# Solving the delta rule's triangular systems for eight matrices at once, in 64-row quarters of TensorE

## The chip, the cores and the metric

The kernel runs on one core of one Trainium2 chip. The metric is the device time of one execution in microseconds (us). A NeuronCore has a matrix engine (TensorE, in the profile PE for its matmuls and PEld for the loading of its weights), VectorE (DVE), ScalarE (ACT) and GpSimd (POOL); SyncE (SP) starts most of the transfers. Matmul results go to PSUM, which is cut into eight banks of 512 fp32 columns.

## The reference

The program is a small decoder trunk: two layers, 512 tokens, model width 1024, fp32. Each layer normalizes x, projects it by one large matrix, and sends the parts to three mixers: a gated spatial MLP, a sliding-window attention, and a gated DeltaNet of 4 heads of 128 channels. Their outputs are projected, gated and added; a SwiGLU MLP follows. The part that the change touches is the DeltaNet. Cut to what matters, with chunks of C = 64 tokens:

```python
q, k, v, beta, g = to_chunks(q), to_chunks(k), to_chunks(v), to_chunks(beta), to_chunks(g)
gc = jnp.cumsum(g, axis=-1)
decay = jnp.exp(jnp.where(tril, gc[..., :, None] - gc[..., None, :], -jnp.inf))
k_beta = k * beta[..., None]
lower = jnp.where(strict, jnp.einsum('nbhid,nbhjd->nbhij', k_beta, k) * decay, 0.0)
a_mat = lower + jnp.eye(C, dtype=jnp.float32)
rhs = jnp.concatenate([v * beta[..., None], k_beta * jnp.exp(gc)[..., None]], axis=-1)
sol = lax.linalg.triangular_solve(a_mat, rhs, left_side=True, lower=True, unit_diagonal=True)
u_c, w_c = sol[..., :hd], sol[..., hd:]
...
def step(state, xs):
    qd, wc, uc, at, kd, cd = xs
    v_new = uc - jnp.einsum('bhcd,bhde->bhce', wc, state)
    o_c = jnp.einsum('bhcd,bhde->bhce', qd, state) + jnp.einsum('bhij,bhje->bhie', at, v_new)
    state = state * cd[..., None, None] + jnp.einsum('bhcd,bhce->bhde', kd, v_new)
    return state, o_c
```

So per head and chunk there is a unit lower triangular matrix to be inverted, and then a scan over the chunks that carries a 128x128 state.

## The kernel before, in words

**Tiling.** Tokens stand in 4 chunks of 128 (twice the reference's chunk; the result is the same by algebra). The large projections run on TensorE with 512-column outputs in four PSUM banks with the tag mm. Their fp32 operands are split into a high and a low fp32r part (hH and hL, wh and wl), and three matmuls stand for one. ScalarE makes wh from a loaded weight tile st, VectorE makes wl. Everything small (DeltaNet, attention, transposes) runs as plain fp32 matmuls into four other banks with the tag px.

**The DeltaNet.** A class Delta stands for two of the four heads (gi is 0 or 1). decay and keys build la for each chunk: la[:, hl, 0, :] is the strictly lower matrix of head hl, transposed, 128x128; keys also scales k into kd, on VectorE (line 632). queries and values prepare q and v. blocks, in one go for all 16 matrices of the layer (4 heads, 4 chunks), fetches their 16x16 diagonal blocks by a DMA into nx, inverts these on VectorE (prd and tb) and spreads the result over the partitions as cols. solve (lines 673 to 727) then builds the inverse of one pair of heads in one chunk. It starts from the 16x16 blocks in Tm and, transposed, in Uc, and has two levels, 16 and 32. At each level TensorE multiplies la by Tm for two heads into one px bank; VectorE multiplies that by a mask lmt and writes ys; TensorE multiplies ys by the other matrix; VectorE subtracts. All these matmuls are 128x128, so the two 64-row diagonal blocks go through one matmul, half of whose entries are zero. A last step joins the 64-row blocks, by 64x64 matmuls (lines 712 to 723). The result U goes to scan, which waits for it chunk by chunk: dv is updated from the state S (lines 747 to 752), U times dv gives y, which is written over la, and kd times y gives the next S.

**What sets the order.** TensorE's order is fixed by a planner (class Issue, lines 50 to 165). Each piece of work is a stream, a generator with a rank; `run` continues the first stream, by rank, whose time has come. A stream's time comes when its last result would be ready by the planner's own costs plus a latency LAT of 0.7; the large projections have rank 10 and fill what is left. Streams wait for one another by named events: a solve waits for blocks{l}, the scan for U{l}{gi}{c}. Two Delta streams (gi 0 and 1) run solve side by side, so their matmuls stand in TensorE's order as pairs. On the other engines the order is the scheduler's, by priorities; `soon()` raises that of the solve's evacuations.

The solve streams are started by these lines:

```python
for e in d:
    issue.spawn(2, dn_stream(e))
    issue.spawn(3, e.solves())
    issue.spawn(1, qv_stream(e))
```

Of the kernel before, what the change touches and what calls it, by code (L numbers as in the profile page):

```python
# [10 lines left out]
F32 = mybir.dt.float32  # L11
# [3 lines left out]
ALU = mybir.AluOpType  # L15
# [3 lines left out]
P = 128  # L19
# [8 lines left out]
HEAD_PERM = [0, 4, 1, 5, 2, 6, 3, 7]  # L28
LEVELS = [16, 32]


# [7 lines left out]
DENSE = 10  # L39
PAD = 48  # L40
SOON = 200
# [122 lines left out]
def hybrid_kernel(ctx, tc, x0, pos, wi, wkv, wb, wo, wg, wd, gn, convw, lngb, sguw, sgub,  # L164
# [33 lines left out]
    def cst(shape, name, dt=F32):  # L198
        return const.tile(shape, dt, name=name, tag=name)
# [58 lines left out]
    for b in (16, 32, 64):  # L258
        t = cst([P, P], f"blk{b}") if b == 16 else tmpc.tile([P, P], F32, name=f"blk{b}")
        v = t.rearrange("p (n b) -> p n b", b=b)  # L260
        nc.gpsimd.affine_select(v, ones.rearrange("p (n b) -> p n b", b=b), pattern=[[-b, P // b], [0, b]],
                                compare_op=ALU.is_ge, fill=0.0, base=0, channel_multiplier=1)
        nc.gpsimd.affine_select(v, v, pattern=[[b, P // b], [0, b]],
                                compare_op=ALU.is_ge, fill=0.0, base=b - 1, channel_multiplier=-1)
        blk[b] = t

    lmt = {}
    for b in LEVELS:
        t = cst([P, P], f"lmt{b}")
        nc.gpsimd.tensor_tensor(t, blk[2 * b], blk[b], ALU.subtract)  # L270
        nc.gpsimd.tensor_tensor(t, t, tri_gt, ALU.mult)
        lmt[b] = t
    blk16 = blk[16]

# [153 lines left out]
    def layer(l, norm, first=None):  # L428
# [110 lines left out]
        def h2(t):  # L539
            return t.rearrange("p (h i) -> p h i", h=2)  # L540

        def bc(m):
            return m.unsqueeze(1).broadcast_to([P, 2, P])

        def hb():
            return bank("px")[:, :256]
# [5 lines left out]
        def hs(hl):  # L552
            return slice(hl * P, (hl + 1) * P)
# [3 lines left out]
        def soon():  # L557

            return tc.high_priority(SOON)

        class Delta:
# [10 lines left out]
            def wt(self, shape, name, bufs=1):  # L572
                return self.wk.tile(shape, F32, tag=name, name=nm(name), bufs=bufs)
# [4 lines left out]
            def decay(self):  # L578

                for c in range(NCH):  # L580
                    col = self.col(c)
                    lg = self.wt([P, 2, P], "Tm", 2)
                    for hl in range(2):
# [13 lines left out]
            def keys(self):  # L597
# [4 lines left out]
                for c in range(NCH):  # L602
# [28 lines left out]
                    for hl in range(2):  # L631
                        nc.vector.tensor_scalar(self.kd[hl][:, tk], pt[:, hs(hl)], kds[:, hl:hl + 1], None, ALU.mult)
                    yield
# [26 lines left out]
            def values(self):  # L660
                for hl in range(2):
                    yield f"v{l}{2 * self.gi + hl}"
                for c in range(NCH):
# [7 lines left out]
                    yield  # L671

            def solve(self, c):

                wt, la = self.wt, self.la[c]
                m = 8 * self.gi + 2 * c
                with soon():
                    Tm, U = wt([P, 2, P], "Tm", 2), wt([P, 2, P], "Uc", 2)
                    for i, (eng, t) in enumerate(((nc.vector, Tm), (nc.gpsimd, U))):
                        eng.tensor_tensor(t.rearrange("p a (n b) -> p a n b", b=16),  # L680
                                          cols[0][:, i, m:m + 2].unsqueeze(2).broadcast_to([P, 2, 8, 16]),
                                          blk16.rearrange("p (n b) -> p n b", b=16).unsqueeze(1)
                                          .broadcast_to([P, 2, 8, 16]), ALU.mult)
                yield
                for b in LEVELS:
                    py = hb()
                    for hl in range(2):
                        nc.tensor.matmul(py[:, hs(hl)], lhsT=la[:, hl, 0, :], rhs=Tm[:, hl, :], start=True, stop=True)
                    with soon():
                        ys = wt([P, 2, P], "ys", 2)  # L690
                        nc.vector.tensor_tensor(ys, h2(py), bc(lmt[b]), ALU.mult)
                    yield
                    pz = hb()
                    if b == 16:
                        for hl in range(2):
                            nc.tensor.matmul(pz[:, hs(hl)], lhsT=U[:, hl, :], rhs=ys[:, hl, :], start=True, stop=True)
                        with soon():
                            nc.vector.tensor_tensor(Tm, Tm, h2(pz), ALU.subtract)
                            U = wt([P, 2, P], "U", 6)
                            for hl in range(2):  # L700
                                nc.vector.transpose(U[:, hl, :], Tm[:, hl, :])
                    else:
                        for hl in range(2):
                            nc.tensor.matmul(pz[:, hs(hl)], lhsT=ys[:, hl, :], rhs=U[:, hl, :], start=True, stop=True)
                        with soon():
                            nc.vector.tensor_tensor(U, U, h2(pz), ALU.subtract)
                            for hl in range(2):
                                nc.vector.transpose(Tm[32:64, hl, 0:32], U[0:32, hl, 32:64])
                    yield
                py = hb()  # L710
                for hl in range(2):
                    nc.tensor.matmul(py[64:128, hl * 64:(hl + 1) * 64], lhsT=la[0:64, hl, 0, 64:128],
                                     rhs=Tm[0:64, hl, 0:64], start=True, stop=True)
                with soon():
                    ys = wt([P, 2, P], "ys", 2)
                    nc.scalar.copy(ys[64:128, :, 0:64], py[64:128, 0:128].rearrange("p (h i) -> p h i", h=2))
                yield
                pz = hb()
                for hl in range(2):
                    nc.tensor.matmul(pz[0:64, hl * 64:(hl + 1) * 64], lhsT=ys[64:128, hl, 0:64],  # L720
                                     rhs=U[64:128, hl, 64:128], start=True, stop=True)
                with soon():
                    nc.vector.tensor_scalar(U[0:64, :, 64:128], pz[0:64, 0:128].rearrange("p (h i) -> p h i", h=2),
                                            -1.0, None, ALU.mult)
                self.U[c] = U
                issue.set(f"U{l}{self.gi}{c}")
                yield

            def solves(self):
                for c in range(NCH):  # L730
                    if c >= 3:
                        yield f"o{l}{self.gi}{c - 3}"
                    yield f"blocks{l}"
                    yield from self.solve(c)

            def scan(self):
                yield f"z{l}"
                for c in range(NCH):
# [63 lines left out]
                    issue.set(f"o{l}{self.gi}{c}")  # L802
                    yield

        def blocks(wk):
# [315 lines left out]
        for e in d:  # L1121
            issue.spawn(2, dn_stream(e))
            issue.spawn(3, e.solves())
            issue.spawn(1, qv_stream(e))
        issue.spawn(4, keys_done())
        issue.spawn(5, attn_prep())
# [266 lines left out]
```

## Time and profile before

| | us |
|---|---|
| median of 3 runs | 1744.66 (1744.47 to 1744.91) |
| profiled execution, its own time | 1743.22 |
| span of the profiled execution | 1741.5 |
| TensorE matmuls, busy | 1718.5 |
| VectorE, busy | 875.7 |
| ScalarE, busy | 638.5 |
| GpSimd, busy | 413.4 |

The span goes from the first to the last instruction of the profiled execution; its mean granted TensorE clock was 0.998 of full speed. Durations of matmuls in the timeline include the end of the pipeline, which lies beside the next matmul; what one costs is the distance to the next start. In a group, out<-in names the tiles without their numbers, and "px<-Tm,la" is a matmul that reads Tm and la into a px bank. Behind the "|" of a group stand its busy time, the mean duration in ns, and the idle time of the engine ahead of it with what ended most of that. An fp32 matmul of the solve has two records in the trace.

### The profile page before, as it was taken

Reading aid. Unit: us, or ns where it says so; the run is one execution under the profiler, and the core shown is the slowest. Engines: PE = TensorE matmul, PEld = TensorE weight load, DVE = VectorE, ACT = ScalarE, POOL = GpSimd, SP = SyncE. Lnnn points to the kernel's source line nnn. Section 1 sums busy time; section 2 is a strip of 40 time slices with the busy share of each in tenths; the row PEclk is TensorE's granted clock in tenths of the full one; section 3 lists DMA queues with packets and bytes.
Section 4 is the critical chain, followed back from the end, with each engine's and each line's share of the span. In section 5 each row is a group of like instructions: output and inputs, shape, how many; then the busy total and the mean of one; then the engine's idle time right before and its main releaser. Section 6 shows DMA issues by size and latency. Waiting matters only on the chain.

```text
span 1741.5 us, 22004 instructions
## 1 busy us (share of the span) xinstructions
PE 1718.5 (99%) x8324; PEld 1421.1 (82%) x8324; DVE 875.7 (50%) x1744; ACT 638.5 (37%) x1182; POOL 413.4 (24%) x447
## 2 busy tenths in 40 slices
PE   9999999999999999999999998999999999999998
PEld 8888778888888888888888886788888888888886
DVE  7695875454443333332266948744444433333224
ACT  7454553322333222222244455533233422222212
POOL 2424221011223333310014143210212233333000
PEclk9999999999999999999999999999999999999999
DMA  5222112222352222234332220122224434444222
GB/s 173 92 95 85 37 43 75 96 97 97 109 172 96 97 98 97 94 114 130 119 117 97 89 85 25 56 85 87 95 97 134 162 109 122 121 121 157 97 97 85
DMA packets 73115, 176.57 MB, mean 101 GB/s; under 512 B 24945, under 2 KB 25201, under 8 KB 73009
## 3 DMA queue, kind: packets, MB, share of 16 engines
q1 hardware_dynamic: 71184, 170.71, 30.3%
q0 software_dynamic: 1248, 3.41, 0.7%
q8 instruction: 65, 1.06, 0.3%
q10 hardware_dynamic: 576, 1.05, 0.2%
q14 instruction: 42, 0.34, 0.1%
HBM read 162.03 MB, written 13.11 MB: 101 GB/s over the span
## 4 chain that ended last, share of the span: by engine, by line
PE 93%; DVE 4%; DMA 1%; POOL 1%; ACT 1%; issue 1%; SPq 0%; POOLq 0%; ACTq 0%; DVEq 0%
PE mm L119 81%; PE px L119 12%; DMA nx<-blkscr 1%; DVE wl L119 0%; POOL of L119 0%; DVE zg L119 0%; DVE U L119 0%; DMA blkscr<-la 0%; DVE pr L119 0%; DVE gv L119 0%; DVE ys L119 0%; DVE gw L119 0%; DMA x<-in_x 0%; POOL pr L119 0%; DVE S L119 0%
## 5 line engine op out<-in xcount | busy, mean ns | idle before, releaser
L119 ACT CAST wh<-st 128x1024 fp32r<-128x1024 f32 (+2 forms) x286 | 295.8, 1034 | 834.0 <-PE mm L119 629.9
L119 PE MATMUL mm<-hH,wh 128*128 128x512 f32 x1344 | 532.9, 397 | 0.0
L119 PE MATMUL mm<-hH,wl 128*128 128x512 f32 x1344 | 523.8, 390 | 0.0
L119 PE MATMUL mm<-hL,wh 128*128 128x512 f32 x1344 | 523.2, 389 | 0.0
L119 DVE TENSOR_TENSOR wl<-st,wh 128x1024 fp32r<-128x1024 f32 (+2 forms) x286 | 353.1, 1235 | 220.2 <-ACT wh L119 209.5
L119 PEld LDWEIGHTS mm<-hH,wl 128*128 128x128 f32 x1344 | 252.2, 188 | 53.3
L119 PEld LDWEIGHTS mm<-hH,wh 128*128 128x128 f32 x1344 | 252.4, 188 | 52.9 <-issue 2.2
L119 PEld LDWEIGHTS mm<-hL,wh 128*128 128x128 f32 x1344 | 252.6, 188 | 51.1 <-issue 1.4
L119 POOL TENSOR_TENSOR s<-s,rep 128x512 f32<-128x512 f32 x44 | 77.3, 1756 | 162.3 <-ACT s L119 162.3
L119 POOL TENSOR_TENSOR aL<-s,aH 128x512 fp32r<-128x512 f32 x44 | 77.4, 1760 | 156.5 <-ACT aH L119 156.5
L119 POOL TENSOR_TENSOR gt<-gt,gt 128x512 f32<-128x512 f32 x32 | 48.8, 1524 | 267.8 <-DVE gt L119 267.8
L119 DVE TENSOR_TENSOR s<-mm,s 128x512 f32<-128x512 f32 x44 | 30.4, 692 | 143.9 <-PE mm L119 137.1
L119 DVE TENSOR_TENSOR s<-mm,rep 128x512 f32<-128x512 f32 x44 | 30.4, 692 | 138.3 <-PE mm L119 121.2
L119 DVE TENSOR_TENSOR gt<-mm,rep 128x512 f32<-128x512 f32 x48 | 33.1, 690 | 105.0 <-PE mm L119 105.0
L119 PE MATMUL mm<-wh,hH 128*128 128x512 f32 (+1 forms) x208 | 83.6, 402 | 0.1
L119 PE MATMUL mm<-wh,hL 128*128 128x512 f32 (+1 forms) x208 | 80.2, 386 | 0.6 <-DVE hL L119 0.6
L119 PE MATMUL mm<-wl,hH 128*128 128x512 f32 (+1 forms) x208 | 79.6, 383 | 0.0
L119 PE MATMUL mm<-brH,wh 128*128 128x512 f32 x192 | 74.7, 389 | 0.0
L119 PE MATMUL mm<-brL,wh 128*128 128x512 f32 x192 | 74.7, 389 | 0.0
L119 PE MATMUL mm<-brH,wl 128*128 128x512 f32 x192 | 74.7, 389 | 0.0
L119 PE MATMUL mm<-aH,wh 128*128 128x512 f32 x176 | 68.5, 389 | 0.0
L119 PE MATMUL mm<-aL,wh 128*128 128x512 f32 x176 | 68.5, 389 | 0.0
(285 smaller groups left out, 2494.9 us busy)
## 6 DMA issues: line engine op xcount, KB each, us to landing
st<-in_wi SPq DMA_DIRECT2D x104, 512.0 KB, 3.2
st<-in_wg SPq DMA_DIRECT2D x88, 512.0 KB, 3.3
st<-in_wb SPq DMA_DIRECT2D x24, 512.0 KB, 3.2
st<-in_wt SPq DMA_DIRECT2D x22, 512.0 KB, 3.3
st<-in_wo SPq DMA_DIRECT2D x16, 512.0 KB, 3.3
st<-in_wd SPq DMA_DIRECT2D x16, 512.0 KB, 3.5
xscr<-xt SPq DMA_DIRECT2D x24, 256.0 KB, 2.0
xt<-xscr SPq DMA_DIRECT2D x24, 256.0 KB, 2.9
```

The lines of the kernel that those rows point to most:

```text
L119: return f(*args, **kw)
```

## The change

The method solve of one pair of heads in one chunk goes; a function solves(b) takes its place, with b = 0 for the chunks 0 and 1 and b = 1 for the chunks 2 and 3, each for all four heads: eight matrices. The two 64-row diagonal blocks of a matrix are stacked on the partitions 0 to 63 and 64 to 127 of tiles of 64 columns per matrix (Tc, Uc and ys are [128, 8, 64]), and a step is 16 matmuls of 64x64 into one px bank of 512 columns. They alternate between the upper left quarter of the array (partitions 0 to 63 in and out) and the lower right one (64 to 127). The evacuation of a step is one VectorE operation of 128x512 (for U two of 64 partitions), and the two last ones, ys and U, are ScalarE's. Batch 1 waits for the event that batch 0 is done. The masks lmt and blk16 become 64 columns wide. Beside that, kd is scaled on ScalarE, the decay's tile has a name of its own (lg), a padding tile grows from 48 to 112 columns, and the program is built with a scratch of 8192 for dynamic DMAs.

```diff
@@ keys: the scaling of kd
-                        nc.vector.tensor_scalar(self.kd[hl][:, tk], pt[:, hs(hl)], kds[:, hl:hl + 1], None, ALU.mult)
+                        nc.scalar.activation(self.kd[hl][:, tk], pt[:, hs(hl)], AF.Copy, scale=kds[:, hl:hl + 1])
@@ the solve: Delta.solve and Delta.solves go (printed above), and this comes
+        def solves(b):
+            chunks = (2 * b, 2 * b + 1)
+            heads = [(4 * ci + 2 * e.gi + hl, e, c, hl) for ci, c in enumerate(chunks) for e in d for hl in range(2)]
...
+            yield f"blocks{l}" if b == 0 else f"U{l}11"
+            Tc, Uc = wt([P, 8, H], "Tc"), wt([P, 8, H], "Uc")
+            with soon():
+                for i, (eng, t) in enumerate(((nc.vector, Tc), (nc.gpsimd, Uc))):
+                    for ci, c in enumerate(chunks):
+                        for e in d:
+                            h0, m = 4 * ci + 2 * e.gi, 8 * e.gi + 2 * c
+                            eng.tensor_tensor(t[:, h0:h0 + 2, :].rearrange("p a (n b) -> p a n b", b=16),
...
+            yield
+            U = wt([P, 8, P], "U", 2)
+            nc.gpsimd.memset(U[H:P, :, 0:H], 0.0)
+            for b_ in LEVELS:
+                py = b8()
+                for k, e, c, hl in heads:
+                    for a in (slice(0, H), slice(H, P)):
+                        nc.tensor.matmul(py[a, k, :], lhsT=e.la[c][a, hl, 0, a], rhs=Tc[a, k, :], start=True, stop=True)
+                ys = wt([P, 8, H], "ys")
+                with soon():
+                    nc.vector.tensor_tensor(ys, py, bc8(lmt[b_]), ALU.mult)
+                yield
+                pz = b8()
+                if b_ == 16:
+                    for k, e, c, hl in heads:
+                        for a in (slice(0, H), slice(H, P)):
+                            nc.tensor.matmul(pz[a, k, :], lhsT=Uc[a, k, :], rhs=ys[a, k, :], start=True, stop=True)
+                    with soon():
+                        nc.vector.tensor_tensor(Tc, Tc, pz, ALU.subtract)
+                        Uc = wt([P, 8, H], "Uc")
+                        nc.vector.transpose(Uc.rearrange("p h i -> p (h i)"), Tc.rearrange("p h i -> p (h i)"))
+                else:
+                    for k, e, c, hl in heads:
+                        for a in (slice(0, H), slice(H, P)):
+                            nc.tensor.matmul(pz[a, k, :], lhsT=ys[a, k, :], rhs=Uc[a, k, :], start=True, stop=True)
+                    with soon():
+                        for a in (slice(0, H), slice(H, P)):
+                            nc.vector.tensor_tensor(U[a, :, a], Uc[a, :, :], pz[a, :, :], ALU.subtract)
+                        for k in range(8):
+                            nc.vector.transpose(Tc[32:H, k, 0:32], U[0:32, k, 32:H])
+                yield
+            py = b8()
+            for k, e, c, hl in heads:
+                nc.tensor.matmul(py[H:P, k, :], lhsT=e.la[c][0:H, hl, 0, H:P], rhs=Tc[0:H, k, :], start=True, stop=True)
+            ys = wt([P, 8, H], "ys")
+            with soon():
+                nc.scalar.copy(ys[H:P, :, :], py[H:P, :, :])
+            yield
+            pz = b8()
+            for k, e, c, hl in heads:
+                nc.tensor.matmul(pz[0:H, k, :], lhsT=ys[H:P, k, :], rhs=U[H:P, k, H:P], start=True, stop=True)
+            with soon():
+                nc.scalar.activation(U[0:H, :, H:P], pz[0:H, :, :], AF.Copy, scale=-1.0)
+            for ci, c in enumerate(chunks):
+                for e in d:
+                    e.U[c] = U[:, 4 * ci + 2 * e.gi:4 * ci + 2 * e.gi + 2, :]
+                    issue.set(f"U{l}{e.gi}{c}")
+            yield
@@ the streams
         for e in d:
             issue.spawn(2, dn_stream(e))
-            issue.spawn(3, e.solves())
             issue.spawn(1, qv_stream(e))
+        for b in range(2):
+            issue.spawn(3, solves(b))
@@ the program
-    nc = bacc.Bacc("TRN2", target_bir_lowering=False, num_devices=1)
+    nc = bacc.Bacc("TRN2", target_bir_lowering=False, num_devices=1, dynamic_dma_scratch_size=8192)
```

Since the planner counts the new work, the order of TensorE changes, and with it that of the other engines. Three places of the orders follow; "x4" is four instructions of the same form in a row.

The first place is TensorE at the first solve step of layer 0; kT,qT are the attention's logits of its first chunk, ident,aq are transposes. Before:

```order
L119 MATMUL px_1744<-ident,aq_365 128x128 x4
L119 MATMUL px_1751<-Tm_1730,la_670 128x128 x2
L119 MATMUL px_1756<-Tm_1734,la_676 128x128 x2
L119 MATMUL mm_1680<-wh_1719,hH_108 128x512
L119 MATMUL mm_1680<-wl_1720,hH_108 128x512
...
L119 MATMUL px_1767<-ys_1754,Uc_1731 128x128 x2
L119 MATMUL px_1774<-ys_1759,Uc_1735 128x128 x2
L119 MATMUL px_1787<-kT_1185,qT_1749 128x128
```

After the change:

```order
L120 MATMUL px_1780<-kT_1194,qT_1760 128x128
L120 MATMUL px_1781<-kT_1194,qT_1760 128x128
L120 MATMUL px_1820<-Tc_1739,la_679 64x64 x4
L120 MATMUL px_1820<-Tc_1739,la_685 64x64 x4
L120 MATMUL px_1820<-Tc_1739,la_727 64x64 x4
L120 MATMUL px_1820<-Tc_1739,la_733 64x64 x4
L120 MATMUL px_1839<-kT_1194,qT_1760 128x128
L120 MATMUL px_1840<-kT_1194,qT_1760 128x128
L120 MATMUL px_1839<-kT_1194,qT_1760 128x128
L120 MATMUL px_1840<-kT_1194,qT_1760 128x128
L120 MATMUL px_1877<-ident,aq_374 128x128 x4
L120 MATMUL mm_1687<-wh_1885,hH_126 128x512
```

In place of two pairs of 128x128 matmuls there are 16 of 64x64, and they stand between two groups of kT,qT.

The second place is VectorE in layer 0, where blocks begins: nx is the operation that needs the DMA of the 16x16 blocks, dq the last step of a head's convolution that gives a query tile. Before:

```order
L119 SCALAR_TENSOR_TENSOR cv_1280<-pre_1278,cw_228,cv_1280 128x509
L119 SCALAR_TENSOR_TENSOR cv_1321<-pre_1319,cw_228,cv_1321 128x511
L119 TENSOR_SCALAR ssq_1344<-ssq_1344 128x2
L119 TENSOR_SCALAR nx_1363<-nx_1363 128x256
L119 SCALAR_TENSOR_TENSOR dq_1202<-pre_1278,cv_1280 128x512
L119 TENSOR_TENSOR prd_1369<-tb_1366,nx_1363 128x1
L119 SCALAR_TENSOR_TENSOR cv_1321<-pre_1319,cw_228,cv_1321 128x510
L119 TENSOR_REDUCE tb_1366<-prd_1369 128x1
```

After the change:

```order
L120 SCALAR_TENSOR_TENSOR la_825<-px_1265,sj_1277,la_825 128x128 x2
L120 SCALAR_TENSOR_TENSOR dq_1211<-pre_1287,cv_1289 128x512
L120 TENSOR_TENSOR pre_1328<-mm_1297,rep_521 128x512
L120 TENSOR_TENSOR wl_1519<-st_1517,wh_1518 128x1024
L120 SCALAR_TENSOR_TENSOR cv_1330<-pre_1328,cw_237,cv_1330 128x511
L120 TENSOR_SCALAR ssq_1353<-ssq_1353 128x2
L120 SCALAR_TENSOR_TENSOR la_679<-px_1348,sj_905,la_679 128x128
L120 SCALAR_TENSOR_TENSOR cv_1330<-pre_1328,cw_237,cv_1330 128x510
L120 SCALAR_TENSOR_TENSOR la_679<-px_1348,sj_905,la_679 128x128
L120 SCALAR_TENSOR_TENSOR cv_1330<-pre_1328,cw_237,cv_1330 128x509
L120 TENSOR_SCALAR nx_1372<-nx_1372 128x256
```

dq stood behind nx and stands ahead of it now; cv and la of the next tile do too.

The third place is ScalarE at the end of the first solve of layer 0, from the evacuation ys to what follows U; gv and gw belong to the spatial MLP, la is y of the scan. Before, where U of that solve is VectorE's:

```order
L119 COPY ys_1931<-px_1928 64x2x64
L119 COPY ys_1936<-px_1933 64x2x64
L119 COPY pT_1941<-px_1938 128x256
L119 CAST wh_2298<-st_2297 128x1024
L119 COPY pT_1960<-px_1957 128x256
L119 COPY pT_1965<-px_1962 128x256
L119 ACTIVATE gv_2206<-mm_1678,rst_409 128x512
L119 COPY la_670<-px_1979 128x2x128
```

After the change:

```order
L120 CAST wh_2631<-st_2630 128x1024
L120 COPY ys_2098<-px_2089 64x512
L120 COPY qT_2087<-px_2082 128x512
L120 ACTIVATE gw_2163<-gw_2163 128x512
L120 ACTIVATE gv_2168<-mm_1689,rst_418 128x512
L120 ACTIVATE gv_2175<-mm_1690,rst_418 128x512
L120 ACTIVATE U_1818<-px_2138 64x8x64
L120 ACTIVATE pr_2107,rsum_2113<-pr_2107,ng_2110 128x256 x2
L120 COPY la_679<-px_2189 128x2x128
```

qT, gw and two gv stand between ys and U now, and the scan's la behind U.

## Rows read from the trace of the kernel before

**Rows 1.** The page, parts 1 and 4: busy time, and the chain by engine.

```profile
PE 1718.5 (99%) x8324; PEld 1421.1 (82%) x8324; DVE 875.7 (50%) x1744; ACT 638.5 (37%) x1182; POOL 413.4 (24%) x447
...
PE 93%; DVE 4%; DMA 1%; POOL 1%; ACT 1%; issue 1%; SPq 0%; POOLq 0%; ACTq 0%; DVEq 0%
```

**Rows 2.** TensorE's groups in the solve, by form.

```profile
L119 PE MATMUL px<-Tm,la 128*128 128x128 f32 x128 | 18.3, 278 | 1.2 <-DVE mxv L119 1.2
...
L119 PE MATMUL px<-U,ys 128*128 128x128 f32 x64 | 9.5, 287 | 0.5 <-DVE ys L119 0.3
...
L119 PE MATMUL px<-Tm,la 64*64 64x64 f32 x64 | 5.8, 226 | 0.0
```

**Rows 3.** TensorE's timeline around three bursts: start us, length us, instruction.

```profile
166.31 0.39 PE L119 MATMUL mm<-wh,hL 128*128 128x512 f32 x1
...
167.01 0.39 PE L119 MATMUL mm<-wh,hL 128*128 128x512 f32 x1
167.23 1.05 PE L119 MATMUL px<-U,ys 128*128 128x128 f32 x8
...
168.82 0.40 PE L119 MATMUL mm<-wh,hH 128*128 128x512 f32 x1
...
197.18 0.39 PE L119 MATMUL mm<-hH,wl 128*128 128x512 f32 x1
197.49 0.68 PE L119 MATMUL px<-Tm,la 64*64 64x64 f32 x8
...
198.91 0.40 PE L119 MATMUL mm<-hH,wh 128*128 128x512 f32 x1
...
251.18 0.39 PE L119 MATMUL mm<-hH,wl 128*128 128x512 f32 x1
251.50 0.44 PE L119 MATMUL px<-Tm,la 64*64 64x64 f32 x4
...
252.68 0.39 PE L119 MATMUL mm<-hH,wh 128*128 128x512 f32 x1
```

**Rows 4.** TensorE's waits: us in total, times, longest us.

```profile
PE px L119 <- DVE Tm L119: 5.8, 4, 2.6
PE px L119 <- DVE mxv L119: 3.5, 4, 1.1
PE px L119 <- DVE dq L119: 2.9, 2, 1.5
```

**Rows 5.** TensorE's timeline, two bursts in half tiles.

```profile
204.96 1.08 PE L119 MATMUL px<-pT,vt 128*64 128x256 f32 x8
...
229.12 1.13 PE L119 MATMUL px<-kT,qT 64*128 64x256 f32 x8
```

**Rows 6.** VectorE's timeline at nx, with the idle time before.

```profile
119.86 0.29 DVE L119 TENSOR_SCALAR nx<-nx 128x256 f32<-128x256 f32 x1 [2.56 <-DMA nx<-blkscr]
120.07 0.69 DVE L119 SCALAR_TENSOR_TENSOR dq<-pre,cv 128x512 f32<-128x512 f32 x1
```

**Rows 7.** TensorE's timeline, two of its waits.

```profile
120.81 0.33 PE L119 MATMUL px<-ident,dq 128*128 128x128 f32 x1 [1.47 <-DVE dq L119]
...
185.04 0.41 PE L119 MATMUL px<-ident,pr 128*128 128x128 f32 x2 [2.55 <-DVE Tm L119]
```

**Rows 8.** Stretches: busy us of PE, PEld, DVE, ACT, POOL; granted clock.

```profile
90.00:100.00 10.00, 10.00 (x54) 8.36 (x53) 9.93 (x27) 4.20 (x12) 2.50 (x3) 1.00 0.34 120
185.00:190.00 5.00, 4.96 (x14) 2.52 (x15) 3.71 (x21) 2.79 (x10) 0.75 (x2) 0.66 0.02 5
```

**Rows 9.** Groups of VectorE and ScalarE, by form.

```profile
L119 DVE TENSOR_TENSOR gt<-mm,rep 128x512 f32<-128x512 f32 x48 | 33.1, 690 | 105.0 <-PE mm L119 105.0
...
L119 DVE TENSOR_TENSOR ys<-px,lmt 128x256 f32<-128x256 f32 x32 | 13.2, 421 | 9.3 <-PE px L119 9.2
...
L119 ACT COPY pT<-px 128x512 f32<-128x512 f32 x24 | 13.9, 579 | 11.6 <-PE px L119 11.3
...
L119 ACT ACTIVATE gw<-gw 128x512 f32<-128x512 f32 x16 | 10.0, 626 | 4.6 <-DVE gw L119 4.4
```

More of the change, by code (lines that the diff above doesn't have):

```diff
@@ L29 @@
 LEVELS = [16, 32]
+H = 64
 CI_QKV, CI_U, CI_Q, CI_V, CI_Z, CI_G = 0, 12, 16, 20, 24, 28
@@ L39 @@
 DENSE = 10
-PAD = 48
+PAD = 112
 SOON = 200
@@ L258, in hybrid_kernel @@
     for b in (16, 32, 64):
-        t = cst([P, P], f"blk{b}") if b == 16 else tmpc.tile([P, P], F32, name=f"blk{b}")
+        t = tmpc.tile([P, P], F32, name=f"blk{b}")
         v = t.rearrange("p (n b) -> p n b", b=b)
@@ L268, in hybrid_kernel @@
     for b in LEVELS:
-        t = cst([P, P], f"lmt{b}")
+        t = tmpc.tile([P, P], F32, name=f"lmt{b}")
         nc.gpsimd.tensor_tensor(t, blk[2 * b], blk[b], ALU.subtract)
         nc.gpsimd.tensor_tensor(t, t, tri_gt, ALU.mult)
-        lmt[b] = t
-    blk16 = blk[16]
+        lmt[b] = cst([P, H], f"lmt{b}")
+        for a in range(2):
+            nc.gpsimd.tensor_copy(lmt[b][a * H:(a + 1) * H, :], t[a * H:(a + 1) * H, a * H:(a + 1) * H])
+    blk16 = cst([P, H], "blk16")
+    for a in range(2):
+        nc.gpsimd.tensor_copy(blk16[a * H:(a + 1) * H, :], blk[16][a * H:(a + 1) * H, a * H:(a + 1) * H])
     amask = cst([P, 2, P], "amask")
@@ L581, in decay @@
                     col = self.col(c)
-                    lg = self.wt([P, 2, P], "Tm", 2)
+                    lg = self.wt([P, 2, P], "lg", 2)
                     for hl in range(2):
@@ L671, in values @@
                     yield
[L673 to L734, printed above, removed]
             def scan(self):
@@ L803, in scan, with wt, bc8, b8 @@
                     yield
+        def solves(b):
+            chunks = (2 * b, 2 * b + 1)
+            heads = [(4 * ci + 2 * e.gi + hl, e, c, hl) for ci, c in enumerate(chunks) for e in d for hl in range(2)]
+            def wt(shape, name, bufs=1):
+                return dw.tile(shape, F32, tag=name, name=nm(name), bufs=bufs)
+            def bc8(m):
+                return m.unsqueeze(1).broadcast_to([P, 8, H])
+            def b8():
+                return bank("px").rearrange("p (h i) -> p h i", h=8)
+            yield f"blocks{l}" if b == 0 else f"U{l}11"
[6 more added lines that the diff above has]
+                            eng.tensor_tensor(t[:, h0:h0 + 2, :].rearrange("p a (n b) -> p a n b", b=16),
+                                              cols[0][:, i, m:m + 2].unsqueeze(2).broadcast_to([P, 2, 4, 16]),
+                                              blk16.rearrange("p (n b) -> p n b", b=16).unsqueeze(1)
+                                              .broadcast_to([P, 2, 4, 16]), ALU.mult)
+            yield
[46 more added lines that the diff above has]
+            yield
```

## The prediction

> **What bounds the kernel now.** I read the page first. TensorE is busy for 1718.5 of 1741.5 us, and the chain of waits that ended last is 93% TensorE [rows 1]. So an edit is worth what it does to the time that TensorE spends on its own instructions, plus what it does to the few places where TensorE stands. VectorE is busy half of the time.
>
> Second I read the groups of instructions on TensorE. Every fp32 matmul of the solve stands as two records there. The solve of the two layers is 256 records of 128 columns by a 128x128 array (128 reading la, 64 reading U, and as many reading Uc) and 128 records of 64 columns by 64x64, half of them reading la [rows 2]. Their mean durations (278 and 226 ns) overlap the next record and are no cost. The cost is the spacing, and the timeline gives it. Big fp32r matmuls follow one another every 0.227 us or so (166.31 to 167.23 are four places, 0.92). Between the start of the last big one ahead of an 8-record solve burst (167.01) and the fourth behind it (168.82) lie 1.81 us; I take 0.91 of it for the four places; the burst costs 0.90 us, or 0.113 per record. For 64x64 the same subtraction gives 198.91-197.18-0.91 = 0.82 us for 8 records and 252.68-251.18-0.91 = 0.59 for 4: 0.24 for four more, so 0.06 per record, and 0.35 for going into the small mode and out again, 0.17 a switch [rows 3].
>
> Third I asked who TensorE waited for: VectorE, 12.2 us in three rows. 2.9 of it are two waits for dq, one in each layer; 9.3 lie in the stretch where solve, scan and attention share the four px banks [rows 4].
>
> **The change part by part, on TensorE.** Per layer and batch of eight matrices each of the four level steps issues 16 fp32 matmuls of 64x64, 32 records. Two layers, two batches and four steps give 512 records in place of the 256 wide ones. The last two steps stay at 128 records over the program. The removed records cost 256 x 0.113 = 28.9 us.
>
> The new ones alternate between the upper left and the lower right quarter of the array. Before only ever uses one quarter in a burst (0.06 per record), so the trace shows no two quarters at once; the bounds are these. If the two quarters do not overlap, 512 x 0.06 = 30.7 us. If they overlap fully, a pair takes the place of one: 256 x 0.06 = 15.4 us. The nearest rows are two kinds of half tile. Eight records of pT,vt alternate two column halves and take 1.08 us to the end of the last; a 256-column fp32 record alone would take a place of twice the 0.113 of a 128-column one, so 1.8 in all. Eight records of kT,qT alternate two row halves: 1.13 us [rows 5]. Take off the 0.17 for a switch and both run at two at once. I take 15.4: a gain of 13.5 us.
>
> The halves differ from the quarters in one respect. The two column halves write one PSUM bank; the two row halves write two. The change's two quarters are different row tiles writing one bank, though different partitions of it. The Trainium skill speaks against that: TensorEngine Tiling (Array Packing), Restrictions and Gotchas, says that different row tiles write to different PSUM banks and cannot access one bank at the same time. By that rule the sum would take 30.7 in place of 15.4; no run so far shows it for tiles that share no partition. It is a rival below.
>
> Switches: the order has 98 changes between the modes of the array in place of 92 (the bursts are longer, but the batched step now splits a burst of kT,qT, see the first order piece). 6 x 0.17 = +1.0 us.
>
> **The wait for dq.** VectorE runs in order, and in before nx stands ahead of dq: it waits 2.56 us for its DMA and dq starts at 120.07, and TensorE, which stood 1.47 us for it, starts at 120.81 [rows 6, 7]. In the changed order dq is ahead of nx in both layers (second order piece). The 2.9 us go if nothing else is late there; if what now stands behind nx (dv, the next pre) is missed instead, nothing goes. Bounds -2.9 and 0; I take -2, nearer to the first, because the wait that is seen is the one whose cause moves.
>
> The move of kd puts 16 instructions a layer from VectorE to ScalarE. From 90 to 100 us, where several kd of the first layer stand, TensorE is busy throughout and ScalarE 42% of the time [rows 8], so I count the move in this term alone. If that cover went, ScalarE's casts of the weights would be late by one or two such instructions, each under the 0.58 us of a copy four times as wide [rows 9], and TensorE with them.
>
> **VectorE and ScalarE in the solve.** The evacuations get wider and fewer: 32 multiplications ys of 421 ns become 8 of some 0.69 (the time of a 128x512 operation on PSUM), likewise the subtractions; the two last evacuations are ScalarE's at about the 0.58 of pT each [rows 9]. VectorE's load falls, which is worth nothing by itself. What counts is the hand-over: TensorE's result, one evacuation, TensorE again. It grows from 0.42 to 0.69 us plus two signals (0.05 by dq's end at 120.76 and TensorE's start; I allow 0.2 each, 1.1 in all), but there are 24 of them in the program where there were 48 for pairs of heads. Against it, I find three places in the new order with too little ahead of a step. At the first step the multiplication ys stands behind a weight split of 1024 columns and two masked maxima pr, all asked for at about the same time, and TensorE has kT,qT, four transposes and six big matmuls behind the burst, some 2.5: I put 0.6. At the end of a batch, ScalarE has qT, gw and two gv between ys and U (0.58 + 0.63 + 2 x 0.69, as gt, = 2.59 us [rows 9], third order piece), and U itself takes 0.58, while TensorE has a burst of 16 small records (16 x 0.06 + 0.35 = 1.3) and four transposes of one record each (0.45): 1.4 short. In the second batch the scan's four updates dv stand behind two zg and ys on VectorE: 6 of at most ys's 0.42 and one of 0.69, 3.2 us, while TensorE has kT,qT (0.9) behind the last S,dk: at most 2.3, I put 2.2. With 0.8 for the rest that is 5 us a layer, 10 in all, against 9.3 and some small waits before, so no gain. Bounds: all of the old waits gone (-9.3) and twice as many (+9).
>
> One of the old waits, 2.55 us at 185.04, was followed by a stretch at the lower clock: 185 to 190 us has a granted clock of 0.66, so some 3.4 us at 1.2 GHz instead of 2.4 ((1 - 0.66) x 5 / 0.5), which costs 1.7 us [rows 7, 8]. It can go, stay or come twice. With that I put the whole stretch at -0.5.
>
> The POOL work (Uc in four pieces, two memsets of U) is as large as before and its engine is mostly idle. The memsets run ahead of the first use. The constants and the smaller DMA scratch cost nothing on TensorE; if the scratch held a POOL transfer back, nx would be later, and its cover is that it lands at 119.86 [rows 6], 47 us before the solve burst of [rows 3].
>
> **Sum.** -13.5 + 1.0 - 2.0 - 0.5 = -15.0 us from the profiled execution's 1743.2, 1.7 of which lie around its span. The median of the runs is 1.4 above it, so 1744.7 - 15.0 = 1729.7: I say 1730.
>
> **Rivals.**
> - The quarters run one after the other, by the bank or because the instructions come no faster: the quickest steady stream of loads and matmuls here is one instruction in some 0.03 us (16 in a burst of 8 records), and a pair in 0.06 would need four in that time. Then 30.7 - 28.9 + 1.0 - 2.0 - 0.5 = -0.7: 1744, no change. For it: no row of more than one quarter, and the rule above. Against it: the halves. Half overlap (three quarters of 30.7, 23.0) gives 1737.
> - The wide steps are exposed: a batch holds one bank for eight matrices, nobody's scan starts before two chunks are solved, and TensorE's order is fixed. If all 24 hand-overs stood open at 1.1 us each, that is +26 on top of the forecast, 1756. It decides once more than about 14 of the 24 are open (15 us). For it: 185.04, where one late VectorE instruction cost 2.55 us. Against it: in the new order nearly every step has big matmuls or other px work of more than 1.1 us behind it.
> - The waits of the stretch go altogether: -9.3 and the clock's -1.7, 1719. For it: VectorE's load falls. Against it: the three places above.
>
> **How the numbers follow.** Forecast 0.56 (its own range 1723 to 1738), half overlap 0.13, no overlap 0.13, exposed steps 0.10, no waits 0.08. The range of 8 in 10 is 1720 to 1745: it leaves out the exposed steps, most of the last case and the far end of the third. A difference of 0.2%, 3.5 us, is what can be told from none. Faster than 1741.2: nearly all of the first (0.55), the last, and most of the second (0.11) with the edge of the third (0.02), 0.76; within: most of the third, and edges, 0.13; slower than 1748.1: 0.11.
>
> **What would show it.** The bursts Tc,la, ys,Uc and Uc,ys should take about 1.3 us for 32 records (16 x 0.06 + 0.35); 2.2 us means no overlap. The two waits for dq should be gone from TensorE's list. The idle time between 150 and 270 us should be near 5 us in each layer; 15 us or more would make the forecast wrong, as would bursts of 2.2 us.

## The result, and the profile after

| | before | after |
|---|---|---|
| median of 4 runs, us | 1744.57 (1743.54 to 1744.91) | 1725.28 (1723.00 to 1728.58) |
| profiled execution, its own time | 1743.22 | 1728.58 |
| span | 1741.5 | 1726.5 |

The ratio of after to before is 0.9892, with a 95% interval of 0.9878 to 0.9906. The prediction was 1730, with a range of 1720 to 1745. The profiled execution of the changed kernel is the slowest of its four; its rows say why (below).

The page first: TensorE's busy time and the chain, as in [rows 1].

```profile
PE 1706.7 (99%) x8580; PEld 1410.4 (82%) x8580; DVE 852.8 (49%) x1624; ACT 648.0 (38%) x1206; POOL 414.8 (24%) x457
...
PE 95%; DVE 2%; ACT 1%; POOL 1%; issue 0%; DMA 0%; SPq 0%; POOLq 0%; ACTq 0%; DVEq 0%
```

TensorE is still the bound. It is busy for 11.8 us less. Next its groups in the solve, as in [rows 2].

```profile
L120 PE MATMUL px<-Tc,la 64*64 64x64 f32 x320 | 13.8, 222 | 0.0
...
L120 PE MATMUL px<-ys,Uc 64*64 64x64 f32 x128 | 4.6, 221 | 0.0
L120 PE MATMUL px<-Uc,ys 64*64 64x64 f32 x128 | 4.6, 221 | 0.0
L120 PE MATMUL px<-U,ys 64*64 64x64 f32 x64 | 4.6, 221 | 0.0
```

The 256 wide records have become 512 quarter records (256 of the 320 of Tc,la, and the 128 each of ys,Uc and Uc,ys); 64 of Tc,la and the 64 of U,ys are the last two steps. The busy times say more than in [rows 2]: records that lie side by side are counted once, so 128 of ys,Uc take 4.6 us, and so do the 64 of U,ys, which all stand in one quarter. The timeline shows it for one burst between big matmuls, as in [rows 3].

```profile
166.74 0.39 PE L120 MATMUL mm<-wh,hL 128*128 128x512 f32 x1
167.06 1.15 PE L120 MATMUL px<-ys,Uc 64*64 64x64 f32 x32
168.14 0.50 PE L120 MATMUL mm<-wh,hH 128*128 128x512 f32 x1
...
168.95 0.39 PE L120 MATMUL mm<-wh,hH 128*128 128x512 f32 x1
```

From 166.74 to the fourth big start behind the burst, 168.95, lie 2.21 us; less 0.91 that is 1.30 for 32 records, as forecast (1.3). A burst of 32 alternating records takes 1.08 us to the next start (167.06 to 168.14), and so does a burst of 16 in one quarter (for example 186.51 to 187.58 in the next fence). In the single records of the trace the starts of this burst stand in pairs, 6 or 7 ns apart, with some 52 ns from a pair to the next; in the burst of one quarter they are 58 or 59 ns apart. Two quarters run side by side.

The waits, as in [rows 4], and the timeline where TensorE waited in layer 0 at the end of the first batch:

```profile
PE px L120 <- DVE U L120: 2.5, 1, 2.5
PE px L120 <- ACT pT L120: 1.9, 2, 1.2
PE px L120 <- POOL pr L120: 1.5, 3, 0.6
PE px L120 <- DVE mxv L120: 1.1, 1, 1.1
PE px L120 <- DVE ys L120: 1.1, 1, 1.1
...
PE px L120 <- DVE ng L120: 0.7, 1, 0.7
```

```profile
186.51 1.14 PE L120 MATMUL px<-U,ys 64*64 64x64 f32 x16
187.58 0.66 PE L120 MATMUL px<-ident,pr 128*128 128x128 f32 x4
189.35 1.90 PE L120 MATMUL px<-dv,U 128*128 128x128 f32 x8 [1.11 <-DVE mxv L120]
...
191.48 0.63 PE L120 MATMUL mm<-hL,wh 128*128 128x512 f32 x1
191.91 0.63 PE L120 MATMUL mm<-hH,wl 128*128 128x512 f32 x1
```

```profile
185.76 0.58 ACT L120 COPY ys<-px 64x512 f32<-64x512 f32 x1
186.37 0.58 ACT L120 COPY qT<-px 128x512 f32<-128x512 f32 x1
186.85 0.63 ACT L120 ACTIVATE gw<-gw 128x512 f32<-128x512 f32 x1
187.38 1.26 ACT L120 ACTIVATE gv<-mm,rst 128x512 f32<-128x512 f32 x2
188.52 0.58 ACT L120 ACTIVATE U<-px 64x512 f32<-64x512 f32 x1
```

```profile
189.13 0.08 DVE L120 DVE_READ_ACCUMULATOR2_ANT mxv<- 128x1 f32 x1
```

The row for dq is gone. The wait at 189.35 is the end of the batch of the third order piece, and two operations are late for it. ScalarE's row for U begins at 188.52 and takes 0.58, so U is there at 189.10. The row names mxv, a masked maximum of the attention on VectorE, and its second one ends later still, at 189.21. So an earlier U by itself would have saved some 0.1 us there. The wait of 2.5 us "DVE U" is in layer 1: a pair of kT,qT needs a px bank that VectorE has not emptied.

Behind that gap the big matmuls stand 0.43 us apart (191.48 to 191.91) in place of 0.23. The stretches, as in [rows 8]:

```profile
5.00:12.00 7.00, 5.55 (x26) 4.73 (x25) 5.75 (x9) 5.91 (x10) 5.27 (x13) 0.76 0.89 312
189.00:194.00 5.00, 4.65 (x18) 4.08 (x19) 4.21 (x20) 4.16 (x16) 1.78 (x4) 0.66 0.32 103
1070.00:1075.00 5.00, 5.00 (x27) 3.70 (x26) 2.68 (x19) 3.13 (x13) 2.48 (x5) 0.66 0.00 0
```

Three stretches of this execution have a granted clock below 1: 0.76 over 7 us and twice 0.66 over 5. TensorE was at 1.2 GHz for 2 x (1 - 0.76) x 7 = 3.4 us in the first, and as long in each of the others; that costs half, 3 x 1.7 = 5.1 us. In another run of nearly the same program (kd back on VectorE, below) the same stretches have 1.00, though TensorE has the same gaps of 1.1 and 2.5 us ahead of the last two:

```profile
188.00:193.00 5.00, 4.58 (x24) 3.98 (x25) 4.36 (x20) 4.38 (x16) 1.96 (x4) 1.00 0.32 107
1068.00:1073.00 5.00, 4.86 (x34) 3.76 (x35) 4.30 (x30) 4.28 (x18) 1.64 (x3) 1.00 0.00 0
```

The four executions of the changed kernel, in the order of their times (1723.0, 1724.6, 1726.0, 1728.6), have a mean granted clock of 0.999, 0.998, 0.997 and 0.996. So the profiled execution's 1728.6 is 3.3 above the median for no reason in the code; without the 5.1 it would be 1723.5.

### The profile page after: what moved, and what is told of

Read it like the earlier page. It is cut to its first block, busy times and chain, and to the rows that moved or that the text cites. A ratio compares the mean times of both kernels' runs of the same rounds, so it can differ in the third digit from the quotient of the medians.

```text
span 1726.5 us, 22439 instructions
## 1 busy us (share of the span) xinstructions
PE 1706.7 (99%) x8580; PEld 1410.4 (82%) x8580; DVE 852.8 (49%) x1624; ACT 648.0 (38%) x1206; POOL 414.8 (24%) x457
## 4 chain that ended last, share of the span: by engine, by line
PE 95%; DVE 2%; ACT 1%; POOL 1%; issue 0%; DMA 0%; SPq 0%; POOLq 0%; ACTq 0%; DVEq 0%
PE mm L120 83%; PE px L120 12%; DVE U L120 0%; DVE wl L120 0%; DMA x<-in_x 0%; ACT pr L120 0%; POOL of L120 0%; DVE xf L120 0%; DVE pr L120 0%; DVE S L120 0%; DVE zg L120 0%; DVE Tc L120 0%; ACT wh L120 0%; POOL pr L120 0%; ACT ojk L120 0%
```

## The experiments

Two sums are used below. "Places" of the solve is the time from the start of each solve burst to the next start on TensorE, less idle time, added up over the trace: 42.1 us before and 25.9 after. "Idle" is the time in which TensorE stood, without its first microsecond: 14.7 us before and 11.5 after. Each set of runs has runs of the kernel before beside it, whose medians lie between 1743.75 and 1744.68; a difference of under 1 us between two versions says nothing by itself.

**Alternation.** Is it the two quarters at work at once? The loops over matrices and quarters change places:

```diff
-                for k, e, c, hl in heads:
-                    for a in (slice(0, H), slice(H, P)):
+                for a in (slice(0, H), slice(H, P)):
+                    for k, e, c, hl in heads:
                         nc.tensor.matmul(py[a, k, :], lhsT=e.la[c][a, hl, 0, a], rhs=Tc[a, k, :], start=True, stop=True)
```

(and so at the two other places of the level steps)

> The level steps issue the same 16 matmuls, but first the eight of the upper left quarter and then the eight of the lower right one; everything else is the changed kernel's, the order of the instructions on the other engines too. Theory A (the gain is two quarters at work at once, when their matmuls alternate): neighbours are in one quarter, so a record takes 0.06 us again; the 16 level bursts go from 1.08 us of places to about 2.0, 16 x 0.94 = +15 us, about 1740. Theory B (the gain is fewer and wider evacuations and the waits that went with them): bursts stay at 1.08, the time at 1725.

Measured: 1734.04 (1733.32 to 1735.29), ratio to before 0.9943 [0.9928, 0.9959]. The same burst as in the timeline above:

```profile
164.46 0.39 PE L120 MATMUL mm<-wh,hL 128*128 128x512 f32 x1
164.78 1.90 PE L120 MATMUL px<-ys,Uc 64*64 64x64 f32 x32
166.61 0.50 PE L120 MATMUL mm<-wh,hH 128*128 128x512 f32 x1
```

It takes 1.83 us (164.78 to 166.61) in place of 1.08. Sixteen such bursts give +12.0, and the places of the solve are 37.8, so +11.9. Idle fell by 2.4, since longer bursts cover hand-overs; 12.0 - 2.4 = 9.6, and the medians differ by 8.8. This execution has no stretch at the lower clock while TensorE works; against the changed kernel's 1723.5 without its stretches it is 9.8 longer. Theory A holds; its size was 15 where 12 is right, since 32 records in a row do not cost 32 x 0.06 plus what a switch costs: at the border between the two quarters three pairs start beside each other.

**Two and two.** Within the level steps two matmuls of the upper quarter, then two of the lower:

```diff
+                for i in range(0, 8, 2):
+                    for a in (slice(0, H), slice(H, P)):
+                        for k, e, c, hl in heads[i:i + 2]:
```

> The level steps alternate by two matmuls (four records) of a quarter, not by one. With one after the other in a single quarter, at the border between the two halves of a burst the first three records of the lower quarter start beside the last of the upper one, so TensorE seems to look some records ahead. If it looks three or more ahead, a burst of 32 stays near 1.08 us (up to 1.2); if only neighbours can start together, one record in four overlaps and it takes about 1.6. The span follows: within 2 us of the changed kernel's, or about +8.

Measured: one run, 1726.33; the bursts take 1.12 us.

```profile
164.68 1.20 PE L120 MATMUL px<-ys,Uc 64*64 64x64 f32 x32
165.80 0.50 PE L120 MATMUL mm<-wh,hH 128*128 128x512 f32 x1
```

So it need not be neighbours; a second quarter's records start beside the first's with four records of one quarter in a row; with sixteen in a row only three did, at the border.

**The last two steps.** They use one quarter in the changed kernel. Here the odd matrices go to the other 64 output partitions:

```diff
             for k, e, c, hl in heads:
-                nc.tensor.matmul(py[H:P, k, :], ...
+                a = slice(H, P) if k % 2 == 0 else slice(0, H)
+                nc.tensor.matmul(py[a, k, :], ...
...
-                nc.scalar.copy(ys[H:P, :, :], py[H:P, :, :])
+                nc.scalar.copy(ys[H:P, 0::2, :], py[H:P, 0::2, :])
+                nc.scalar.copy(ys[H:P, 1::2, :], py[0:H, 1::2, :])
```

(and the same for pz and U)

> The last two steps also alternate: the odd matrices write the other 64 partitions of the bank (a column quarter with the same rows), and ScalarE takes each result in two operations of 64 x 256, one of which shifts the partitions back. Theory A for any two quarters: 16 records go from 1.07 us of places to 0.61 (the 16 alternating records of the one-chunk kernel), 8 bursts x 0.46 = -3.7; the evacuations take 2 x 0.37 in place of 0.58, at worst +1.3 where TensorE waits for them: 1722 to 1723. Rival (only the diagonal pair of quarters runs side by side, or TensorE is held by the rows that both read): bursts at 1.07, 1725 or more.

Measured: 1720.88 (1719.93 to 1722.49), 0.9866 [0.9851, 0.9880]: the fastest version, 4.4 us under the changed kernel.

```profile
227.12 0.68 PE L120 MATMUL px<-U,ys 64*64 64x64 f32 x16
227.73 0.50 PE L120 MATMUL mm<-hH,wh 128*128 128x512 f32 x1
```

16 records take 0.61 us (227.12 to 227.73); the places of the solve fell by 3.7 to 22.2, as expected. Idle is 11.9 after 11.5. TensorE's order changed with the planner's costs, so other waits came (1.6 for ScalarE's U, 3.3 for dv) and the 2.5 for a bank went; what the second evacuation costs by itself is not shown.

**The same with VectorE for the odd half of both evacuations**

```diff
-                nc.scalar.copy(ys[H:P, 1::2, :], py[0:H, 1::2, :])
+                nc.vector.tensor_copy(ys[H:P, 1::2, :], py[0:H, 1::2, :])
```

> The last two steps in column quarters as in the run at 1720.9, and the odd half of each of the two evacuations on VectorE, so that the two halves go side by side (0.37 us in place of 0.74 in a row). If the hand-over is what is left there (waits of 1.6 us for ScalarE's U and 0.4 for ys in that run), -1 to -2, about 1719. Rival: VectorE's own queue (masked maxima, the scan's dv) is later than ScalarE's, as with the whole of U on VectorE (1729.3): 1722 to 1726.

Measured: 1726.10 (1723.27 to 1728.40). The rival: idle rose from 11.9 to 13.9, with 3.0 for ys and 4.6 for pT in the list of waits. The two profiled executions are 5.6 apart: 1.9 is this idle time, and 3.4 the clock, 0.83 from 185 to 195 us and 0.66 from 1076 to 1086 (3.4 and 6.8 us at 1.2 GHz) where the run at 1720.9 has one stretch of 3.4.

**The batch.** One chunk (four matrices) at a time, and one pair at a time as before the change:

```diff
-            chunks = (2 * b, 2 * b + 1)
+            chunks = (b,)
...
-        for b in range(2):
+        for b in range(NCH):
             issue.spawn(3, solves(b))
```

> The same quarters in alternation, but a batch is one chunk, four matrices: four batches a layer, bursts of 16 records in the level steps and of 8 in the last two. Theory A with the price of a switch: 32 level bursts of 16 x 0.03 + 0.35 = 0.83 in place of 16 of 1.31, +5.6; 16 last bursts of 8 x 0.06 + 0.35 = 0.83 in place of 8 of 1.31, +2.8; so +8.4, about 1734, the work itself unchanged. Theory B' (long hand-overs and late scans are what remains as idle time): evacuations of 256 columns hand over sooner and the scan starts after one chunk, so the 11 us of waits in the two layers shrink and the time is 1725 or less.

Measured: 1737.10 (1735.89 to 1738.49), +11.8 on the changed kernel.

```diff
-            heads = [(4 * ci + 2 * e.gi + hl, e, c, hl) for ci, c in enumerate(chunks) for e in d for hl in range(2)]
+            heads = [(hl, e0, c0, hl) for hl in range(2)]
...
-        for b in range(2):
-            issue.spawn(3, solves(b))
+        for e in d:
+            issue.spawn(3, solves(e))
```

> Quarter tiles without the batch: a solve is again one pair of heads in one chunk, as before, with its two diagonal blocks stacked and its matmuls alternating between the quarters; kd on ScalarE. The two streams still stand next to each other in TensorE's order, so a burst is 16 records, the same as with batches of one chunk. Theory A with the price of a switch: 32 level bursts at 0.83 (16 x 0.03 + 0.35) in place of the 0.90 of the wide ones, -2.4, and -2.9 for dq: about 1738 to 1739, close to the 1737.1 of one chunk at a time; the batch of eight is worth the remaining 12. Rival (the quarters alone carry the gain): about 1727.

Measured: 1729.53 (1728.40 to 1730.39), 0.9914 [0.9899, 0.9929]. Here my price failed by 9 us. The places of the solve are 31.2 in this kernel and 30.8 with one chunk, the same; so the quarters without the batch carry 10.9 of the 16.2 us. I had charged each of the 32 bursts two switches of 0.17. But the order has 127 changes of mode in place of 92, 35 more and not 64: half of the 32 bursts stand beside kT,qT or pT,vt, where the array changes mode anyway. And a wide burst costs more by places away from big matmuls: 1.0 us on the mean (42.1 less 10.2 for the last steps, by 32), where the one of [rows 3] takes 0.81, from 167.23 to this row of before:

```profile
168.04 0.48 PE L119 MATMUL mm<-wh,hH 128*128 128x512 f32 x1
```

Ahead of kT,qT it is 0.98, and where TensorE waits in a burst or behind it 1.06 to 1.26, since the end of the last record then lies beside nothing. A burst of 16 quarter records takes 0.61 between big matmuls and ahead of kT,qT alike. What makes one chunk 7.6 us slower than one pair is not the bursts. The longest of its waits, in the view of TensorE's waits:

```profile
PE px L120 <- POOL pr L120: 3.4, 2, 3.0
PE px L120 <- DVE Tc L120: 3.4, 1, 3.4
```

One of them is in the last chunk of layer 0, at 252.06, behind a queue on VectorE (brL, u, a weight split of 1.22 us, then U and Tc); both are followed by a stretch at 1.2 GHz (granted clock 0.66 over 250 to 260 us and 0.57 over 1109 to 1117). The two profiled executions are 5.5 apart: idle is 2.0 more than with one pair, and the clock costs 6.8 in place of 3.4. The order that the planner found for this batch is worse; that smaller batches as such are is not shown.

**kd alone**, taken back in the changed kernel and put into the one before. TensorE's order is unchanged in both:

```diff
-                        nc.scalar.activation(self.kd[hl][:, tk], pt[:, hs(hl)], AF.Copy, scale=kds[:, hl:hl + 1])
+                        nc.vector.tensor_scalar(self.kd[hl][:, tk], pt[:, hs(hl)], kds[:, hl:hl + 1], None, ALU.mult)
```

> The changed kernel with the scaling of kd on VectorE again, as before; TensorE's order is unchanged by this. Theory K (the move of kd alone is what put dq ahead of nx): VectorE's order has nx ahead of dq again, the two waits of 1.47 and 1.40 us for dq return, +2.9, about 1728. Rival: the waits went by the solve's new order and kd is worth nothing: 1725, no wait for dq on TensorE.

> The kernel before with only the scaling of kd moved to ScalarE; TensorE's order is unchanged. Theory K: the two waits for dq go, 1744.6 - 2.9 = 1741.7. Rival: what stands behind nx now is late in their place, or the casts on ScalarE are: 1744.6 or more.

Measured: taken back, 1726.37 (1726.01 to 1728.84), +1.1; put into the kernel before, 1741.06 (1738.68 to 1744.36, 11 runs), 0.9981 [0.9972, 0.9990], so -3.1. VectorE with kd on it, then in the changed kernel:

```profile
119.47 0.29 DVE L120 TENSOR_SCALAR nx<-nx 128x256 f32<-128x256 f32 x1 [2.52 <-DMA nx<-blkscr]
119.67 0.69 DVE L120 SCALAR_TENSOR_TENSOR dq<-pre,cv 128x512 f32<-128x512 f32 x1
```

```profile
115.34 0.69 DVE L120 SCALAR_TENSOR_TENSOR dq<-pre,cv 128x512 f32<-128x512 f32 x1 [0.16 <-ACT pre L120]
...
122.72 0.29 DVE L120 TENSOR_SCALAR nx<-nx 128x256 f32<-128x256 f32 x1 [2.02 <-DMA nx<-blkscr]
```

With kd, dq stands behind nx and TensorE waits for it:

```profile
PE px L120 <- DVE dq L120: 3.5, 2, 2.1
```

Without, dq runs 7 us ahead of nx. Theory K holds in the traces of both. In the changed kernel the medians show only 1.1 of the 3.5, within the spread that the clock gives it; the profiled executions show 2.9 (1726.4, with no stretch at the lower clock while TensorE works, against the 1723.5).

**The last evacuation**, U, on VectorE again:

```diff
-                nc.scalar.activation(U[0:H, :, H:P], pz[0:H, :, :], AF.Copy, scale=-1.0)
+                nc.vector.tensor_scalar(U[0:H, :, H:P], pz[0:H, :, :], -1.0, None, ALU.mult)
```

> U of the last step is negated by VectorE, as before the change, in place of ScalarE. My prediction put 1.4 us on ScalarE's queue (qT, gw, two gv) between ys and U; the trace of the changed kernel has a wait of 1.1 us of dv,U at 189 us. If that queue is what TensorE waits for, the wait goes: -1.1, about 1724, as far as the new order of what follows brings no other. Rival: dv,U waits for something else (the row names mxv on VectorE), and U stands behind that on VectorE as well: no gain or a loss, 1725 to 1728.

Measured: 1729.27 (1727.74 to 1729.54), +4.0. The rival:

```profile
PE px L120 <- DVE dv L120: 4.0, 4, 1.7
PE px L120 <- DVE ys L120: 2.9, 3, 1.5
...
PE px L120 <- DVE U L120: 1.2, 2, 0.9
```

dv,U still waits for U (0.9), which now stands behind a weight split and two masked maxima on VectorE, and the scan's dv (4.0) and ys (2.9) are late there. TensorE's order changed too. Idle is 13.5, 2.0 more; the granted clock of the four runs is 0.996 and 0.997, and the rest of the 4.0 is not settled.

**The memory edits** in the kernel before:

```diff
-PAD = 48
+PAD = 112
...
-    nc = bacc.Bacc("TRN2", target_bir_lowering=False, num_devices=1)
+    nc = bacc.Bacc("TRN2", target_bir_lowering=False, num_devices=1, dynamic_dma_scratch_size=8192)
```

> The kernel before with only the two edits of memory: the padding tile of 112 columns and the scratch of 8192 for dynamic DMAs. The order of all engines is unchanged. My prediction: nothing on TensorE, 1744.7 and a difference from before inside the noise. Rival: a smaller scratch holds a GpSimd transfer back, nx lands later than 119.86 and TensorE waits longer for dq behind it (more than 1.5 us at one of the two places), 1747 or more.

Measured: 1744.36, ratio 1.0002 [0.9993, 1.0011]; the waits for dq are 1.4 and 1.5. Nothing, as predicted.

**The planner's latency**, in the column-quarter version:

```diff
-LAT = 0.7
+LAT = 0.9
```

> The column-quarter version with the planner's latency LAT at 0.9 in place of 0.7, so TensorE's order puts more other work behind each hand-over; the computation is the same. Theory W (the 8 us of idle time left in the two layers are hand-overs that the planner takes for shorter than they are): idle falls by 2 to 4 us, 1717 to 1719. Rival (they are queues on VectorE and ScalarE that the latency does not describe): waits only move to other places, 1719 to 1724.

Measured: 1748.74 (1747.93 to 1751.35). Neither: idle is 26.5.

```profile
PE px L120 <- DVE la L120: 10.0, 2, 5.3
PE px L120 <- ACT pT L120: 8.3, 6, 3.7
```

The order now asks for values' transposes (ident,dv) right where VectorE's la is 5 us late, in each layer. The waits are only half of the loss. The profiled execution is 29.6 us over that of the run at 1720.9; idle gives 14.6 of it. The clock gives 15.4, since two stretches a layer, behind the waits for la and for pT, have a granted clock below 1:

```profile
150.00:160.00 10.00, 7.71 (x25) 6.20 (x26) 3.61 (x8) 1.25 (x4) 8.38 (x20) 0.66 0.30 105
242.00:254.00 12.00, 9.91 (x64) 7.35 (x64) 6.30 (x25) 7.51 (x25) 2.83 (x4) 0.57 0.19 68
1017.00:1027.00 10.00, 8.22 (x26) 6.57 (x27) 3.10 (x6) 1.25 (x4) 7.88 (x19) 0.66 0.33 107
1109.00:1121.00 12.00, 10.28 (x66) 7.48 (x68) 6.01 (x26) 7.35 (x24) 2.83 (x4) 0.57 0.19 66
```

One constant moves the whole order, and its waits with it.

## Why the prediction was right, step by step

- **The bursts.** Step and mechanism right: 32 alternating records in 1.30 us between big matmuls, 1.3 forecast; alternation undone costs 12. The rival of one bank is out: the two quarters write one PSUM bank in different partitions and run side by side. The Trainium skill's rule on row tiles and one bank (TensorEngine Tiling (Array Packing), Restrictions and Gotchas) does not hold for such tiles here: 1.08 us with both quarters against 1.83 in a row, in the same bank. No run has two row tiles on the same partitions. The same skill's TensorE: Matmul & The Clock Gate (Part 3, Measured speedup vs the span model) puts the span of packed tiles at the duration of one matmul and some 4 ns for each further tile; the starts of a pair lie 6 or 7 ns apart here. The rival of the instruction rate falls too: 32 loads and 32 matmuls in 1.08 us.
- **The size of that term** was too small. Forecast were -13.5 and +1.0 for switches, -12.5. TensorE's whole time less idle is 1718.1 before, and 1702.2 in the run with kd back on VectorE, whose order on TensorE is that of the changed kernel and which has no stretch at the lower clock there. Before has one, worth 1.7 by [rows 8]; so the work fell by 14.2 us: the places of the solve by 16.2, while the rest grew by 2.0, where +1.0 for switches was forecast. Three sizes of the solve were off. The removed records cost 31.9 by places and not 256 x 0.113 = 28.9; 1.6 of it is the end of ten records behind which TensorE waited. The new ones cost 17.3, 16 bursts of 1.08, and not 15.4. And the last two steps, put at no change, fell from 10.2 to 8.6, since their 20 bursts of 8 or 4 records became 8 of 16.
- **dq.** Forecast -2.0 between -2.9 and 0; both waits went (2.9), by the move of kd, and the kernel before gains 3.1 by it alone.
- **The stretch of solve and scan.** Forecast: 10 us of idle time, as much as before. Measured by the timeline between 150 and 266 us and between 999 and 1121: 3.0 and 6.7, so 9.7, after 5.1 and 5.7 in the kernel before (there the second stretch ends at 1129). Of the three places that I named, the end of the first batch waits 1.1 in layer 0 (1.4 forecast) and not at all in layer 1. The forecast has ScalarE's queue ahead of U as the only reason; U was 0.9 late, but VectorE's masked maximum was 1.0 late, and I had not seen it. Near the first step TensorE waits 0.7 and 1.1, but not in front of ys,Uc: ident,aq stands behind ng in layer 0, kT,qT behind ys in layer 1. dv in the second batch waits 0.3 (2.2 forecast, from bounds that were too high). In their place came a bank for kT,qT (2.5) and pT (1.9) in layer 1, which I did not see. The sum was right and its parts were not, so that it came out is luck.
- **The sum.** -14.2 - 2.9 - 1.1 = -18.2 against -15.0 forecast and -19.3 measured. Of the 4.3 that the forecast fell short, the bursts and the other work of TensorE are 1.7, dq 0.9 and the stretch 0.6. The last us is not settled; the granted clock moves single executions by more than that. The rival without overlap was added up wrongly: 30.7 - 28.9 + 1.0 - 2.0 - 0.5 is +0.3 and not -0.7, so 1745.
- **Exposed steps, no waits:** neither came; idle 11.5 after 14.7, of which 2.9 is dq.

## What to carry to other kernels

Small fp32 matmuls that sit on the diagonal of a larger one can run two at a time in opposite quarters of the array, into the two halves of one bank's partitions, if their instructions alternate, and so can two in the same rows and different columns (16 records in 0.61 us in place of 1.07). Price a burst by its neighbours: between full-array work each change of mode costs 0.17; with one pair at a time, where half of the bursts stand beside work in a small mode, that price was too high by 9 us in all, and a full-array burst ahead of such work pays for the change itself (0.98 us in place of 0.81). Look for an operation that waits for a DMA in the middle of an in-order queue: moving 16 small scalings a layer off that queue let dq pass it, worth 3 us here. And where a wait is followed by a lower granted clock, count that too: with the latency at 0.9 it cost as much as the waits.

## What the runs showed that I had not expected

A second quarter's matmuls start beside the first's when the quarters alternate by one matmul (1.08 us for 32 records) or by two (1.12), and little when all of one stand first (1.83). After the same gaps on TensorE of 1.1 and 2.5 us the granted clock fell in one execution (twice 0.66 over 5 us) and not in another (1.00); the four executions of the changed kernel, whose order is fixed, spread over 5.6 us, the faster the higher their granted clock.
